# A streaming encoder layer on one core: output projection and second block finished tile by tile, projection weights loaded in quarters, and rope in four instructions

## The chip, the core and the metric

The kernel runs on one core of a Trainium2 chip. A core has a tensor engine (PE in the profile; PEld is its loading of weights), a vector engine (DVE), a scalar engine (ACT), a GpSimd engine (POOL), and queues for transfers, most of which here are issued by the sync engine (SP). The engines work each in their own order and wait for each other by semaphores. The metric is the device time of one execution in microseconds (us), as the median of several runs.

## What is computed

One step of a one-layer encoder for 1024 prompt rows and 64 sample rows, with 1024 columns, in float32:

```
def macaron_half(x, g, b, w_gate, w_up, w_down):
    return layer_norm(ALPHA * x + 0.5 * swiglu(x, w_gate, w_up, w_down), g, b)

hp = macaron_half(xp, ln1_g, ln1_b, ffn1_w_gate, ffn1_w_up, ffn1_w_down)
qa, ka, va, qi, ki, wi, qb, kb, vb, lfb = project(hp, pos_p, w_in, b_f)   # rope on qa, ka, qi, ki
mp = mixer_prompt(qa, ka, va, qi, ki, wi, qb, kb, vb, lfb)
hp = layer_norm(ALPHA * hp + mp @ w_out, ln2_g, ln2_b)
xp = macaron_half(hp, ln3_g, ln3_b, ffn2_w_gate, ffn2_w_up, ffn2_w_down)
```

The mixer has two groups of heads. Group A picks 256 keys per query by the scores of a small indexer (`relu(q_i . k_i)`, weighted) and attends to them; group B attends causally with a decay. The sample rows go the same way with a cache. The feed-forward blocks are 2816 wide. The outputs are the layer's rows and the new keys and values.

## The kernel before

The rows are held as nine tiles: t = 0 to 7 are 128 prompt rows each, t = 8 the 64 sample rows. To keep float32 precision, every operand of a product is split into a high part, a cast on ACT (L108), and a low part, a subtraction on DVE (L109). A product of two split operands takes three matmuls (high-high, high-low, low-high; `mm`, L113). A tile of rows is turned with PE transposes (`turned`, L124) before it is an operand.

The program runs through these stages: first block part a and part b (to about 741 us of the span), the input projections (to 1083), attention (to 1425), the output projection (to 1528), second block part a (to 2026), second block part b (to the end).

**Blocks.** Part a (`ffn_a`) computes gate and up, part b (`ffn_b`, L591) the down projection. Both use Strassen's scheme with seven half-size products; in part b they are P1 to P7, with P5, P7 and P4 last in that order. The inner dimension of each is cut into six PAIRS of up to 256, the last a half one. `load` (L628) fetches and splits a pair's two operands (`pair`, L621: `mh`, `ml` of the weight, `lh`, `ll` of the hidden rows), two pairs ahead, in rings of three. All tiles t = 0 to 3 use a pair before the next one, except for the last `late` pairs (three in P4, L710), which are done tile by tile, followed by the tile's `evict` (L674). In P4 with `last` (the second block) the eviction adds the product to the row (L662), runs the layer norm (`ln_tail`, L521 to L541) and writes the output.

**Strassen operands.** The second block's operands come from `Strassen.put` (L167): of tile t >= 4 and its partner t - 4 it forms differences (L175, L178, L179, L180 on GpSimd), turns them with PE into `xt` and splits them into T1 to T4 and B22. The partner's rows come back from DRAM into `zt` (`emit_s`, L1991), a 128x1024 buffer of the ring "wl" in the pool `wp`, which the weight splits use as well. The first product of the next stage, on the wide tile `fs`, needs them all.

**Output projection.** `gemm_b` (L432) takes the nine tiles in three groups of three. In a group all tiles go together through the inner dimension but for its tail; then each tile's tail is done in `order` (L435), followed by its first layer norm step. The remaining steps of the three (generators, of five turns each) are queued in `todo` in a fixed interleaving (L479) and are run as the next work is emitted (`pump`).

**Projections.** The 2888 columns of `w_in` are cut into eleven groups, stored as "w" (buffers `wh`, `wl` of the common rings) or as "p" (`iwh`, `iwl` of a pool of their own). `load_w` (L973) loads a group's weight in two parts ("w") or three ("p") into the ring "st" of three 128x1024 buffers and splits each at once (L975 cast on ACT, L976 subtraction). The ring "st" is also used by `rt`, the relu of the indexer scores (`idx_scores`, L1144, on ACT), which PE takes up again. `in_proj` (L1047) runs the tiles of a group and calls for the next group's weights at tile `ahead`. `proj_tile` copies the result to `ot` on ACT (L1040); its handler, run a little later, applies rope (`rope_apply`, L945, six instructions), turns the tile (`tsplit`, L1061, results `tsqb`, `tsqi`, with `hl` L1072 and `ft` L1078) and writes it out. The steps of the top-k search (`topk`, with `tk_bad`, L1327) run in between.

A scheduler orders the instructions of the engines from the order in which the code emits them; `tc.issue_after` pins a place. Queues work in their order: an instruction that waits holds those behind it on its engine.

## Time and profile before

| | us |
|---|---|
| median of 3 runs | 2279.86 (2279.32 to 2284.34) |
| the profiled execution | 2278.69 |
| its span, first to last instruction | 2276.9 |
| granted PE clock, mean | 0.982 of full speed |

The span is that of one execution, read by the hardware profiler. In the views, rows stand as start, duration, engine, line, operation and tiles; a bracket behind a row gives the idle time of the engine before it and what ended it. The table of waits gives the total, the number and the longest of each kind. The table of windows gives busy time by engine, then the granted PE clock, the share of the DMA engines and GB/s. Durations of rows overlap on pipelined engines, so that the step from one start to the next is what a row costs; the chain of waits lists these steps.

### The profile page before, as it was taken

How to read it: one execution, taken by the hardware profiler on the slowest of the kernel's cores; microseconds unless marked ns; L12 is line 12 of the kernel's file. 1: busy time of each engine (PE TensorE's matmuls, PEld its weight loads, DVE VectorE, ACT ScalarE, POOL GpSimd, SP SyncE). 2: the span in 40 equal slices, each digit the busy share in tenths (PEclk: the TensorE clock that was granted, in tenths of full speed). 3: DMA queues.
4: the chain of work that ended last, by engine and by line, in shares of the span. 5: the costliest groups of instructions: out<-in, count | busy, mean ns of one | idle time of the engine just before them, and what ended most of it. 6: DMA issues, size and time to landing. Idle time of an engine off the chain costs nothing.

```text
span 2276.9 us, 33875 instructions
## 1 busy us (share of the span) xinstructions
PE 2186.9 (96%) x11832; PEld 1878.7 (83%) x11832; DVE 1489.8 (65%) x2359; ACT 963.0 (42%) x1776; POOL 906.4 (40%) x1058
## 2 busy tenths in 40 slices
PE   8999999999999999999898999998999999999997
PEld 7888888887888989998897787886888888877886
DVE  4576675556569656686857887675555655654678
ACT  4333333334344356733666787333333333333332
POOL 4556556541011323352546655023564564530011
PEclk9999999999999999999999999998999999999999
DMA  6566544458556343554667533553443443477554
GB/s 200 180 210 217 186 153 148 140 178 304 166 196 208 108 121 118 161 151 133 171 172 202 146 93 113 166 183 113 149 160 117 158 156 117 159 258 237 179 182 152
DMA packets 330297, 379.31 MB, mean 167 GB/s; under 512 B 43440, under 2 KB 226160, under 8 KB 330124
## 3 DMA queue, kind: packets, MB, share of 16 engines
q1 hardware_dynamic: 330122, 377.13, 52.8%
q8 instruction: 94, 1.54, 0.3%
q14 instruction: 81, 0.65, 0.1%
HBM read 256.51 MB, written 120.53 MB: 166 GB/s over the span
## 4 chain that ended last, share of the span: by engine, by line
PE 45%; DVE 5%; issue 1%; ACT 1%; DMA 1%; POOL 1%; SPq 0%; DVEq 0%; ACTq 0%; POOLq 0%
PE fa L114 11%; PE fbP L114 8%; PE fz L114 5%; PE fy L114 3%; PE gb L114 3%; PE pq L114 2%; PE acc L114 2%; PE ip L114 2%; PE pt L1744 2%; PE fs L114 2%; DVE pp L109 1%; PE fbs L114 1%; PE gb_a L114 1%; PE gb_b L114 1%; PE sacc L114 1%
## 5 line engine op out<-in xcount | busy, mean ns | idle before, releaser
L114 PE MATMUL fbP<-ml,lh 128*128 128x512 f32 x616 | 238.6, 391 | 1.5 <-DVE ml L109 1.5
L114 PE MATMUL fbP<-mh,ll 128*128 128x512 f32 x616 | 237.9, 390 | 2.1 <-DVE ll L109 2.1
L108 ACT CAST wh<-wst 128x1024 fp32r<-128x1024 f32 x108 | 113.3, 1052 | 286.6 <-PE fs L114 108.6
L114 PE MATMUL fbP<-mh,lh 128*128 128x512 f32 x616 | 224.2, 392 | 2.6 <-ACT lh L108 1.7
L109 DVE TENSOR_TENSOR wl<-wst,wh 128x1024 fp32r<-128x1024 f32 x108 | 159.5, 1478 | 69.8 <-ACT wh L108 60.6
L331 DVE TENSOR_TENSOR Sl<-S,Sh 128x512 fp32r<-128x512 f32 x160 | 161.8, 1018 | 29.3 <-ACT Sh L330 27.7
L108 ACT CAST lh<-raw 128x1024 fp32r<-128x1024 f32 x84 | 82.4, 981 | 228.4 <-PE fbP L114 195.1
L662 POOL TENSOR_TENSOR zz<-u,zz 128x512 f32<-128x512 f32 x16 | 25.6, 1613 | 379.6 <-DVE u L684 268.8
L330 ACT CAST Sh<-S 128x512 fp32r<-128x512 f32 x160 | 97.4, 618 | 187.4 <-PE fa L114 113.9
L109 DVE TENSOR_TENSOR ll<-raw,lh 128x1024 fp32r<-128x1024 f32 x84 | 100.0, 1191 | 115.2 <-ACT lh L108 115.0
L327 POOL TENSOR_TENSOR S<-wst 128x512 f32<-128x512 f32 x80 | 125.1, 1564 | 113.5 <-DVE Sl L331 52.0
L327 POOL TENSOR_TENSOR S<-wst,S 128x512 f32<-128x512 f32 x40 | 61.6, 1539 | 239.0 <-issue 235.4
L114 PEld LDWEIGHTS fbP<-mh,lh 128*128 128x128 f32 x616 | 115.7, 189 | 27.7 <-ACT lh L108 2.0
L114 PEld LDWEIGHTS fbP<-ml,lh 128*128 128x128 f32 x616 | 115.5, 188 | 27.7 <-DVE ml L109 4.1
L114 PEld LDWEIGHTS fbP<-mh,ll 128*128 128x128 f32 x616 | 115.6, 188 | 26.8 <-DVE ll L109 2.9
L1681 POOL TENSOR_SCALAR e<-e,su 128x128 f32<-128x128 f32 (+7 forms) x128 | 99.4, 789 | 77.3 <-DVE su L1678 61.6
L114 PE MATMUL acc<-pp,vs 128*128 128x256 f32 (+1 forms) x640 | 114.8, 300 | 9.0 <-DVE pp L109 5.6
L109 DVE TENSOR_TENSOR pp<-pt,pp 128x512 fp32r<-128x512 f32 (+1 forms) x160 | 99.1, 631 | 29.4 <-ACT pp L108 28.0
L114 PE MATMUL ip<-iwh,xh 128*128 128x256 f32 (+3 forms) x384 | 114.7, 299 | 2.0 <-ACT o L1043 0.9
L114 PE MATMUL ip<-iwl,xh 128*128 128x256 f32 (+3 forms) x384 | 111.4, 290 | 0.0
L114 PE MATMUL ip<-iwh,xl 128*128 128x256 f32 (+3 forms) x384 | 111.3, 290 | 0.0
L114 PEld LDWEIGHTS acc<-pp,vs 128*128 128x128 f32 x640 | 91.1, 196 | 14.5 <-DVE pp L109 7.9
(507 smaller groups left out, 6746.9 us busy)
## 6 DMA issues: line engine op xcount, KB each, us to landing
wst<-ffn_w_gate SPq DMA_DIRECT2D x88, 256.0 KB
wst<-ffn_w_up SPq DMA_DIRECT2D x88, 256.0 KB
w<-ffn_w_down SPq DMA_DIRECT2D x44, 512.0 KB
raw<-ffn_w_down SPq DMA_DIRECT2D x40, 512.0 KB
wst<-w_out SPq DMA_DIRECT2D x24, 512.0 KB
hd0T<-w SPq DMA_DIRECT2D x44, 256.0 KB
hd0S<-ringz SPq DMA_DIRECT2D x44, 256.0 KB
hd1T<-w SPq DMA_DIRECT2D x44, 256.0 KB
```

The source lines that it names most:

```text
L108: S.copy(hi, src)
L109: V.tensor_tensor(lo, src, f(hi), ALU.subtract)
L114: last_mm[:] = [PE.matmul(out, lhsT, rhs, start=start, stop=stop, skip_group_check=more).ins]
L327: G.tensor_tensor(t, ss[0] if x is None else x, ss[1] if y is None else y, op)
L330: S.copy(hi, t)
L331: V.tensor_tensor(lo, t, f(hi), ALU.subtract)
L662: eng.tensor_tensor(z_of(t, d), acc, z_of(t, d), ALU.add)
L1681: G.tensor_scalar(es[q][:, :n], es[q][:, :n], su2[:, q:q + 1], 1.0, ALU.mult, ALU.mult)
L1744: PE.transpose(pt[:, m * P:(m + 1) * P], e[:, kt * P:(kt + 1) * P], ident)
```

## The change

It has these parts:

- `gemm_b` takes the last group's tiles in the order 0, 1, 2, and queues their layer norm steps tile by tile, five turns each.
- `put` works with `zt` as two halves of 128x512, and with a choice of engine. In `emit_s` the halves come from the ring "ssum" (four buffers of 128x512) by two transfers, and for tiles 6 and 7 the differences are formed on DVE.
- In `ffn_b` with `last`, the first four pairs of P4 are fetched and split into free slots of the large operand pool during P5 (pairs 0, 1) and P7 (pairs 2, 3). In P4 all six pairs are then done tile by tile.
- `rope_apply` multiplies all 16 rotated columns by cosine and by sine at once, and combines them with two instructions.
- `load_w` loads the weights of the nine 256- and 264-column groups in quarters of 128x2x256 (and one small remainder) into the ring "ssum". The loads are issued at once, the splits are kept in `wsp` and emitted one per tile from tile `ahead` + 2 on, the rest before the next group.
- `tsplit` alternates between the two kinds of PSUM tiles in the late groups, and one call of `in_proj` has `ahead` 5.

```diff
@@ -166,3 +166,3 @@
 
-        def put(self, t, z, hf, zt=None):
+        def put(self, t, z, hf, zt=None, E=G):
             if t == 8:
@@ -174,11 +174,11 @@
                 self.set("B22", t, turned(t, z, 1))
-                G.tensor_tensor(zt[:, 0:512], z[:, 0:512], zt[:, 0:512], ALU.subtract)
-                self.set("T1", t, turned(t, zt, 0))
+                E.tensor_tensor(zt[0], z[:, 0:512], zt[0], ALU.subtract)
+                self.set("T1", t, turned(t, zt[0], 0))
             else:
-                G.tensor_tensor(z[:, 0:512], z[:, 512:1024], z[:, 0:512], ALU.subtract)
-                G.tensor_tensor(z[:, 512:1024], z[:, 512:1024], zt[:, 0:512], ALU.subtract)
-                G.tensor_tensor(zt[:, 512:1024], zt[:, 512:1024], z[:, 512:1024], ALU.subtract)
+                E.tensor_tensor(z[:, 0:512], z[:, 512:1024], z[:, 0:512], ALU.subtract)
+                E.tensor_tensor(z[:, 512:1024], z[:, 512:1024], zt[0], ALU.subtract)
+                E.tensor_tensor(zt[1], zt[1], z[:, 512:1024], ALU.subtract)
                 self.set("T2", t, turned(t, z, 1))
                 self.set("T3", t, turned(t, z, 0))
-                self.set("T4", t, turned(t, zt, 1))
+                self.set("T4", t, turned(t, zt[1], 0))
 
@@ -434,3 +434,3 @@
             skew = tail if g == 2 else 2
-            order = (2, 0, 1) if g == 2 else (0, 1, 2)
+            order = (0, 1, 2)
             acc = []
@@ -478,3 +478,5 @@
                         pass
-            for j in (0, 0, 0, 1, 1, 1, 0, 0, 2, 2, 2, 1, 1, 2, 2):
+            turns = (0, 0, 0, 0, 0, 1, 1, 1, 1, 1, 2, 2, 2, 2, 2) if g == 2 else \
+                (0, 0, 0, 1, 1, 1, 0, 0, 2, 2, 2, 1, 1, 2, 2)
+            for j in turns:
                 if not last or g < 2:
@@ -623,3 +625,7 @@
                 st = fetch(src, n, tags[0])
-                hl = [pool.tile([P, 1024], F32R, tag=tg, name=tg, bufs=3) for tg in tags[1:]]
+                if pool is None:
+                    both = slot8("tl" + tags[1]).rearrange("p (s c) -> p s c", s=2)
+                    hl = [both[:, 0], both[:, 1]]
+                else:
+                    hl = [pool.tile([P, 1024], F32R, tag=tg, name=tg, bufs=3) for tg in tags[1:]]
                 split(hl[0][:, :n * 512], hl[1][:, :n * 512], st[:, :n * 512])
@@ -627,4 +633,8 @@
 
+            NP = len(PAIRS)
+            FAR = 4 if last else 0
+            far = [steps.index(("P4", q)) for q in range(FAR)]
+
             def load(i):
-                if i >= len(steps):
+                if i >= len(steps) or i in ops:
                     return
@@ -632,4 +642,5 @@
                 A, B = OPS[p]
-                ops[i] = pair(w_src(B, q), q, ("st", "mh", "ml"), hb_)
-                ops[i] += pair(hd[A][q][0:PAIRS[q][1]].rearrange("k p c -> p k c"), q, ("wl", "lh", "ll"), hb_)
+                pool = None if i in far else hb_
+                ops[i] = pair(w_src(B, q), q, ("st", "mh", "ml"), pool)
+                ops[i] += pair(hd[A][q][0:PAIRS[q][1]].rearrange("k p c -> p k c"), q, ("wl", "lh", "ll"), pool)
 
@@ -709,3 +720,3 @@
             for p in OPS:
-                late = 3 if p == "P4" else 2
+                late = (NP if last else 3) if p == "P4" else 2
                 acc = [sm(f"fb{p}_{t}") for t in range(4)]
@@ -715,2 +726,4 @@
                     load(i + q + 2)
+                    if last and p in ("P5", "P7") and q % 3 == 1:
+                        load(far[2 * (p == "P7") + q // 3])
                     if i + q == 2:
@@ -734,3 +747,6 @@
                     for q in range(len(PAIRS) - late, len(PAIRS)):
-                        product(acc[t], t, i + q, False, q == len(PAIRS) - 1)
+                        with ExitStack() as es:
+                            if last and p == "P4" and t and q == 0:
+                                es.enter_context(tc.issue_after(last_mm[0]))
+                            product(acc[t], t, i + q, q == 0, q == len(PAIRS) - 1)
                     evict(p, t, acc[t])
@@ -768,3 +784,3 @@
         def put(t, hf):
-            xo.put(t, at[t], hf, at.get(t - 4))
+            xo.put(t, at[t], hf, [at[t - 4][:, c * 512:(c + 1) * 512] for c in range(2)])
             yield
@@ -947,13 +963,11 @@
         v = ot[:r, c0:c0 + nh * HD].rearrange("p (h d) -> p h d", h=nh)
-        x1, x2 = v[:, :, 0:8], v[:, :, 8:16]
-        cosb = rope[:r, t, 0:1, :].to_broadcast([r, nh, 8])
-        sinb = rope[:r, t, 1:2, :].to_broadcast([r, nh, 8])
-        a, b = (att.tile([P, 4, 8], F32, tag=n, name=n, bufs=2) for n in ("ra", "rb"))
+        x12 = v[:, :, 0:16].rearrange("p h (s d) -> p h s d", s=2)
+        cosb, sinb = (rope[:r, t, q:q + 1, :].rearrange("p (a b) d -> p a b d", a=1).to_broadcast([r, nh, 2, 8])
+                      for q in range(2))
+        a, b = (att.tile([P, 4, 2, 8], F32, tag=n, name=n, bufs=2)[:r, :nh] for n in ("ra", "rb"))
         E = rp_[0]
-        E.tensor_tensor(a[:r, :nh], x1, sinb, ALU.mult)
-        E.tensor_tensor(b[:r, :nh], x2, sinb, ALU.mult)
-        E.tensor_tensor(x1, x1, cosb, ALU.mult)
-        E.tensor_tensor(x2, x2, cosb, ALU.mult)
-        E.tensor_tensor(x1, x1, b[:r, :nh], ALU.subtract)
-        E.tensor_tensor(x2, x2, a[:r, :nh], ALU.add)
+        E.tensor_tensor(a, x12, cosb, ALU.mult)
+        E.tensor_tensor(b, x12, sinb, ALU.mult)
+        E.tensor_tensor(x12[:, :, 0], a[:, :, 0], b[:, :, 1], ALU.subtract)
+        E.tensor_tensor(x12[:, :, 1], a[:, :, 1], b[:, :, 0], ALU.add)
 
@@ -972,2 +986,4 @@
 
+    wsp = []
+
     def load_w(c0, n, store, eng):
@@ -977,2 +993,20 @@
 
+        def later(dst):
+            rest = []
+            if n > 256:
+                ex = mp.tile([P, 512], F32, tag="hsh", name="wex")[:, 0:KD * (n - 256)].rearrange(
+                    "p (k c) -> p k c", k=KD)
+                DMA.dma_start(ex, w_in[:, c0 + 256:c0 + n].rearrange("(k p) c -> p k c", p=P))
+                rest.append((slice(0, KD), slice(256, n), ex))
+            for k in range(0, KD, 2):
+                st = mp.tile([P, 512], F32, tag="ssum", name="wst", bufs=4).rearrange("p (k c) -> p k c", k=2)
+                DMA.dma_start(st, w_in[k * P:(k + 2) * P, c0:c0 + 256].rearrange("(k p) c -> p k c", p=P))
+                rest.append((slice(k, k + 2), slice(0, 256), st))
+
+            def one(ks, cs, st):
+                hi, lo = dst(ks, cs)
+                sp2(hi, lo, st)
+
+            wsp.extend(lambda p=p: one(*p) for p in rest)
+
         if store == "w":
@@ -980,9 +1014,7 @@
             for u in range(2):
-                st = wp.tile([P, 1024], F32, tag="st", name="wst")
-                DMA.dma_start(st.rearrange("p (a b) -> p a b", a=4),
-                              w_in[u * 512:(u + 1) * 512, c0:c0 + n].rearrange("(k p) c -> p k c", p=P))
                 wh = wp.tile([P, 1024], F32R, tag="wh", name="wh")
                 wl = wp.tile([P, 1024], F32R, tag="wl", name="wl")
-                sp2(wh, wl, st)
                 us.append((wh, wl))
+            later(lambda ks, cs: [x.rearrange("p (k c) -> p k c", k=4)[:, ks.start % 4:ks.start % 4 + 2, cs]
+                                  for x in us[ks.start // 4]])
 
@@ -995,3 +1027,6 @@
             iwh = pw_[1].tile([P, KD, pw_[2]], F32R, tag="iwh", name="iwh")
-            for k0, kn in ((0, 2), (2, 2), (4, 2), (6, 2)) if hp_[0] is None else ((0, 3), (3, 3), (6, 2)):
+            if hp_[0] is not None and n < 328:
+                later(lambda ks, cs: (iwh[:, ks, cs], iwl[:, ks, cs]))
+            for k0, kn in ((0, 2), (2, 2), (4, 2), (6, 2)) if hp_[0] is None else \
+                    ((0, 3), (3, 3), (6, 2)) if n == 328 else ():
                 if hp_[0] is None:
@@ -1048,4 +1083,8 @@
         in_weights(gi)
+        while wsp:
+            wsp.pop(0)()
         for t in tiles:
             h = proj_tile(gi, t, mid)
+            if wsp and t > ahead + 1:
+                wsp.pop(0)()
             if t == ahead:
@@ -1060,4 +1099,7 @@
 
+    nts = [0]
+
     def tsplit(r, src, npair, scale, dst, c, cs, eng, name):
-        pt = (big if hp_[0] is pc else sm)("ts" + name)
+        nts[0] += 1
+        pt = (big if hp_[0] is pc and nts[0] % 2 else sm)("ts" + name)
         for q in range(npair):
@@ -1583,3 +1625,3 @@
     in_proj(0, (4, 5, 6, 7), -1)
-    in_proj(1, (4, 5, 6, 7), 6)
+    in_proj(1, (4, 5, 6, 7), 5)
     for gi in range(2, 4):
@@ -1613,2 +1655,4 @@
     hp_[0] = None
+    while wsp:
+        wsp.pop(0)()
     pend_9 = [proj_tile(9, t) for t in range(2)]
@@ -1995,7 +2039,9 @@
         if 4 <= t < 8:
-            zt = wp.tile([P, 1024], F32, tag="wl", name="zt")
-            DMA.dma_start(zt, h2d[t - 4])
-        xo2[0].put(t, z, 0, zt)
+            zt = [mp.tile([P, 512], F32, tag="ssum", name="zt", bufs=4) for _ in range(2)]
+            for c in range(2):
+                DMA.dma_start(zt[c], h2d[t - 4][:, c * 512:(c + 1) * 512])
+        E = V if t >= 6 else G
+        xo2[0].put(t, z, 0, zt, E)
         yield
-        xo2[0].put(t, z, 1, zt)
+        xo2[0].put(t, z, 1, zt, E)
```

What these do to the order of instructions is shown at three places. The first is ACT's order at the switch from the second to the third group of the projections. Before (`rt` is the relu of indexer scores, `iwh` the high part of a weight, `ist` its landing buffer):

```order
L1144 ACTIVATE rt<-iq_1_7380 128x640
L1040 COPY ot<-ip_2_7326 128x256
L1072 ACTIVATE hl<-tskb 128x2x128
L1078 ACTIVATE ft<-tskb 128x256
L975 CAST iwh<-ist 128x3x264 x2
L1144 ACTIVATE rt<-iq_2_7445 128x640
L975 CAST iwh<-ist 128x2x264
L1144 ACTIVATE rt<-iq_3_7462 128x640
```

Now:

```order
L991 CAST iwh<-wex 128x8x8
L991 CAST iwh<-wst 128x2x256 x2
L1114 ACTIVATE hl<-tsqi 128x2x128
L991 CAST iwh<-wst 128x2x256
L1152 CAST kid<-pk_7090 64x128
L991 CAST iwh<-wst 128x2x256
L1186 ACTIVATE rt<-iq_0_7115 128x384
```

The casts of the 264-column weight stood between the relus of 640 columns; now all of them stand ahead of the first relu.

The second place is the end of the operands of the second block, tile 7. Before, POOL formed its differences, with products of the first hidden columns (w) between:

```order
L180 TENSOR_TENSOR zt<-zt,zz 128x512
L245 TENSOR_TENSOR w_17420<-w_17420 128x512
L246 TENSOR_TENSOR w_17420<-w_17420 128x512
L247 TENSOR_TENSOR w_17420<-w_17420 128x512
L175 TENSOR_TENSOR zt<-zz,zt 128x512
L248 TENSOR_TENSOR w_17420<-w_17420 128x512
L178 TENSOR_TENSOR zz<-zz 128x512
L179 TENSOR_TENSOR zz<-zz,zt 128x512
L180 TENSOR_TENSOR zt<-zt,zz 128x512
```

Now they stand on DVE, between the splits (L109) of the turned parts:

```order
L175 TENSOR_TENSOR zt<-zz,zt 128x512
L109 TENSOR_TENSOR T4l<-xt_0_17045,T4h 128x4x128
L178 TENSOR_TENSOR zz<-zz 128x512
L109 TENSOR_TENSOR B22l<-xt_1_17091,B22h 128x4x128
L179 TENSOR_TENSOR zz<-zz,zt 128x512
L109 TENSOR_TENSOR T1l<-xt_0_17099,T1h 128x4x128
L180 TENSOR_TENSOR zt<-zt,zz 128x512
L109 TENSOR_TENSOR T2l<-xt_1_17121,T2h 128x4x128
L109 TENSOR_TENSOR T3l<-xt_0_17128,T3h 128x4x128
```

On SP's queue the copies of the partner's rows (h2d_91 for tile 6, h2d_92 for tile 7) now stand as halves between the writes of the tiles 6 (h2d_95), 7 (h2d_96) and the sample (h2d_97):

```order
L415 DMA wst<-ffn_w_up 128x4x128 x2
L2042 DMA zt<-h2d_91 128x512
L2037 DMA h2d_95<-zz 128x1024
L2042 DMA zt<-h2d_91 128x512
L2037 DMA h2d_96<-zz 128x1024
L2042 DMA zt<-h2d_92 128x512
L2037 DMA h2d_97<-zz 64x1024
L2042 DMA zt<-h2d_92 128x512
```

Before, the copy for tile 7 was one transfer behind all three writes and two loads of weights for the next product.

The third place is the end of the program on DVE. Before, the last steps of the tiles stood interleaved; these are its last rows but the closing branch:

```order
L539 SCALAR_TENSOR_TENSOR zz<-zz,bmv,gb 128x1024
L535 SCALAR_TENSOR_TENSOR bve<-brs,bve 128x1
L534 RECIPROCAL brs<-brs 128x1
L536 TENSOR_SCALAR bve<-bve 128x1
L535 SCALAR_TENSOR_TENSOR bve<-brs,bve 128x1
L537 TENSOR_TENSOR brs<-brs,bve 128x1
L536 TENSOR_SCALAR bve<-bve 128x1
L541 SCALAR_TENSOR_TENSOR zz<-zz,brs,gb 128x1024
L537 TENSOR_TENSOR brs<-brs,bve 128x1
L541 SCALAR_TENSOR_TENSOR zz<-zz,brs,gb 128x1024
```

Now the last rows are the chain of one tile (L673 was L662, L541 was L539, L543 was L541):

```order
L543 SCALAR_TENSOR_TENSOR zz<-zz,brs,gb 128x1024
L673 TENSOR_TENSOR zz<-fbP_3_22176,zz 128x512
L531 BN_STATS bst_22205<-zz 128x6
L532 BN_AGGR bmv<-bst_22205 128x2
L534 TENSOR_SCALAR bve<-bmv 128x1
L541 SCALAR_TENSOR_TENSOR zz<-zz,bmv,gb 128x1024
L536 RECIPROCAL brs<-brs 128x1
L537 SCALAR_TENSOR_TENSOR bve<-brs,bve 128x1
L538 TENSOR_SCALAR bve<-bve 128x1
L539 TENSOR_TENSOR brs<-brs,bve 128x1
L543 SCALAR_TENSOR_TENSOR zz<-zz,brs,gb 128x1024
```

The layer norm of each tile stands whole behind that tile's product, and the one before it is complete ahead of it.

## The prediction

> **What bounds the kernel now.** I read first the busy shares, then the table of what the tensor engine (PE) waited for, then windows around its longest waits, and last the rows inside those windows.
>
> ```profile
> PE 2186.9 (96%) x11832; PEld 1878.7 (83%) x11832; DVE 1489.8 (65%) x2359; ACT 963.0 (42%) x1776; POOL 906.4 (40%) x1058
> PE iq L114 <- ACT rt L1144: 4.7, 2, 4.5
> PE tsqb L1064 <- ACT ft L1078: 3.2, 2, 2.3
> PE xt L129 <- POOL zt L175: 5.6, 1, 5.6
> PE xt L129 <- POOL zz L179: 3.7, 2, 2.7
> PE tkf L114 <- DVE tk_bad L1327: 2.1, 1, 2.1
> ```
>
> PE is busy for 96% of the span: 90 us of 2276.9 are left, and no other engine is near its limit. The change takes no matmul away. It can gain only where PE stands still, or after PE's last matmul. The five waiting rows (total us, times, longest) are the single long stalls in the stretches that the change touches.
>
> ```profile
> core 0: us, PE busy (x) PEld busy (x) DVE busy (x) ACT busy (x) POOL busy (x), PEclk, DMA share, GB/s
> 741.00:1083.00 342.00, 328.14 (x2416) 315.19 (x2415) 230.72 (x517) 170.18 (x388) 127.91 (x315) 0.97 0.46 132
> 839.00:846.00 7.00, 6.17 (x27) 6.17 (x28) 4.96 (x6) 3.77 (x8) 0.00 (x0) 0.51 0.09 30
> 1023.40:1026.80 3.40, 3.40 (x16) 3.40 (x17) 3.40 (x6) 2.25 (x6) 3.39 (x1) 0.51 0.59 175
> 1037.00:1040.40 3.40, 3.16 (x15) 3.16 (x16) 0.54 (x4) 0.00 (x0) 0.00 (x0) 0.50 0.59 155
> 1562.70:1576.30 13.60, 7.15 (x32) 6.75 (x33) 4.71 (x7) 4.60 (x7) 7.21 (x6) 0.50 0.28 103
> 2171.00:2201.60 30.60, 30.60 (x136) 25.35 (x136) 18.95 (x21) 11.07 (x12) 3.46 (x2) 1.00 0.59 193
> 2201.60:2232.00 30.40, 30.03 (x133) 24.52 (x133) 29.93 (x54) 11.87 (x16) 1.92 (x2) 1.00 0.68 227
> 2232.00:2263.50 31.50, 31.31 (x137) 25.26 (x135) 24.19 (x36) 9.45 (x12) 4.07 (x3) 1.00 0.24 81
> 2263.50:2276.90 13.40, 0.00 (x0) 0.00 (x0) 9.82 (x25) 0.41 (x2) 0.00 (x0) 0.59 0.40 157
> ```
>
> The first row is the whole projection stage. Two things are to be seen below it. After each of the long stalls the granted clock is 0.5 for one window of 3.4 us or for several, so a stall costs itself and about half of PE's busy time in that window. And the last 13.4 us hold no matmul at all.
>
> The Trainium skill, "TensorE: Matmul & The Clock Gate", section "What's actually happening", says that the clock halves after a whole idle window of about 3.4 us. The windows here differ: the stalls of 2.3 and 2.1 us at 1023 and 1037 are followed by 0.51 and 0.50. By the page only the stalls of 4.5 and 5.6 us would carry a clock loss, which would make the sum below about 1 us smaller.
>
> **The change part by part.**
>
> *End of the second block (P4 tile by tile).* Rows of the chain of waits (start, us, engine), and two of the timeline:
>
> ```profile
> 2263.10 0.39 PE L114 MATMUL fbP<-mh,ll 128*128 128x512 f32 x1
> 2263.53 0.69 DVE L662 TENSOR_TENSOR zz<-fbP,zz 128x512 f32<-128x512 f32 x1
> 2208.05 1.10 DVE ml L109
> 2262.03 0.59 DVE zz L662
> 2262.81 0.60 DVE bst L529
> 2264.22 0.12 DVE bmv L530
> 2268.93 1.19 DVE zz L539
> 2272.07 1.28 DVE zz L541
> ```
>
> The last matmul ends at 2263.49. Before, the last three pairs of all four tiles run tile by tile, 15 matmuls each, so four layer norms pile up on DVE and its last step ends at 2273.35: a tail of 9.9 us after it. After, a tile's 33 matmuls stand together (33 x 0.227 = 7.5 us), and a tile's DVE chain is add 0.59, statistics 0.60, mean 0.12, four or five small steps of 0.06 to 0.12 (0.37), L539 1.19 and L541 1.28: with start gaps 4.3 us, shorter than a tile's 7.5. Three layer norms go beside matmuls, one stays: 9.9 - 4.3 = **5.6 us less**. The output DMA behind the last step (2273.35 to 2276.9) stays.
>
> Cover: each pair is two splits of 1.10 on DVE (row 2208). Pairs 0 and 1 of P4, split within P7 before, go into P5, which has room (18.95 of 30.6 busy, and 4.4 more). P7 takes pairs 2 and 3 in their place (4.4 for 4.4), and also pairs 4 and the half pair 5, which P4 split for itself before: 29.9 + 3.3 = 33.2 us of DVE work beside 30.4 of PE. P4, rid of 7.7 us of splits, can take the excess of 2.8; pair 5 is needed only at the end of a tile's 7.5 us. If the excess lands on PE all the same, it waits 2.8 us in P4 with a halved window after it, 1.7. So this part lies between 5.6 - 4.5 = 1 and 6 (small steps hidden too); I take 5.5, nearest to the chain's own rows.
>
> *Projections (quarters, deferred splits).* Rows of the timeline, with idle time and releaser in brackets:
>
> ```profile
> 836.11 0.85 ACT L975 CAST iwh<-ist 128x792 fp32r<-128x792 f32 x1 [2.40 <-DMA ist<-w_in]
> 838.32 0.85 ACT L975 CAST iwh<-ist 128x792 fp32r<-128x792 f32 x1 [1.35 <-DMA ist<-w_in]
> 839.08 0.70 ACT L1144 ACTIVATE rt<-iq 128x640 f32<-128x640 f32 x1
> 839.83 1.43 PE L114 MATMUL iq<-kid,qsi 128*128 128x384 f32 x4 [4.54 <-ACT rt L1144]
> 1023.22 1.06 ACT L975 CAST wh<-wst 128x1024 fp32r<-128x1024 f32 x1
> 1023.39 0.69 PE L1064 MATMUL tsqb<-ident,ot 128*128 128x128 f32 x2 [2.33 <-ACT ft L1078]
> 1031.28 0.83 ACT L975 CAST iwh<-ist 128x768 fp32r<-128x768 f32 x1 [2.89 <-DMA ist<-w_in]
> 1032.15 0.96 DVE L976 TENSOR_TENSOR iwl<-ist,iwh 128x768 fp32r<-128x768 f32 x1 [1.19 <-ACT iwh L975]
> 1037.24 0.37 PE L114 MATMUL tkf<-tk_bad,tk_ones 128*128 128x8 f32 x1 [2.06 <-DVE tk_bad L1327]
> ```
>
> At 836 ACT waits in order for a weight's DMA (2.40 + 1.35 us) while the relu of the indexer scores (rt), for which PE waits, stands behind it. The DMA is late because its buffer comes from the same three-buffer ring as rt. After, the weight's DMAs use four other buffers, and its casts stand some 35 ACT rows earlier, ahead of the first rt. The 4.54 us go, with half of the 6.17 busy us of the halved window: 7.6. Late next is rt itself, 0.70 per step.
>
> At 1031 ACT and DVE again wait for a weight part (2.89, 1.19), and the counting step tk_bad comes late behind them. With parts loaded long before, these waits go. 2.06 and 1.6 of clock are the whole stall; I take 2.5, since the count has its own DVE chain.
>
> At 1023 one cast of 1.06 stands ahead of the copy for which PE waits; after, four quarter casts do, half the size each, about 2.1 us in a row: 1 us worse. Bounds: from 1.7 better (its halved window no longer hit) to 2 worse; I take -1, nearest to the cast's row.
>
> Sum 7.6 + 2.5 - 1 = **9**, bounds 2 and 14, the upper with the 2.33 and its window gone. The 36 quarter loads take the place of two or three larger ones per group. They are issued at tile 2 and split from tile 4 on, one per tile; 342 us for ten groups of nine tiles is 3.8 us per tile, so 7.6 us lie between issue and the first split, 19 before the last. The Trainium skill, "DMA: Bandwidth & Descriptors", section "Rules for kernel authors", asks for 1 MiB or more per DMA, and its anatomy section fits 2.0 us fixed per transfer; by an estimate from that page four 256 KB loads in turn would take 10.4 us where two halves took 6.4. That speaks against quarters only if they do not overlap, which is the last rival below.
>
> *Rope with four instructions, alternating PSUM buffers, ahead 5 for 6.* They sit on DVE and POOL beside PE work. PE waits after rope are under 1 us each; I count 0, bounds -2 and +2.
>
> *Output projection end.*
>
> ```profile
> 1549.20 3.66 DVE L541 SCALAR_TENSOR_TENSOR zz<-zz,brs,gb 64x1024 f32<-64x1024 f32 x3
> 1534.78 5.51 PE fa L114 x24
> 1558.48 1.28 POOL zt L180
> 1560.53 4.50 DMA zt<-h2d
> 1566.48 1.13 PE xt L129 x4
> 1570.27 2.82 PE xt L129 x12
> 1573.09 5.30 PE fs L114 x32
> ```
>
> Three layer norms end together (x3, at 1552.86). Then POOL does four subtractions of 1.27 for tile 6, and only when tile 6's buffer is free (1560.53) does tile 7's copy start, 4.50 us of DMA, and four more POOL steps follow. PE idles 5.6 + 2.7 us there, and fs, the next work, starts at 1573.09, its first 3.2 us at half clock (to 1576.3), so 1.6 lost.
>
> After, tile 6 comes about 7 us earlier (its product is complete first and its turns are not interleaved), tile 7 at about 1551; the copies lie in a ring of four halves, so the 4.50 drops out; and the subtractions run on DVE at about 0.6 (the L662 pitch above) instead of 1.27. But DVE has also the splits of the transposed parts, one between every two subtractions (order rows in the section on the change), and the pair of late halves stands in SP's queue behind the sample's write. I put the last subtraction at about 1559.5, the last transposes at 1562. Then 24 fa matmuls, which PE had before to fill its waiting, follow (5.5), and fs starts at about 1569.5: 3.6 us earlier. A halved window is likely still there, since PE waits for DVE's steps in the meantime. **3.5 us less**; bounds -1 (late halves, clock) and 7 (clock whole, DVE quick).
>
> Sum: 5.5 + 9 + 0 + 3.5 = 18. The profiled execution took 2278.69 us (span 2276.9 and 1.8 around it); its place is 1.2 under the median of the runs shown, 2279.86. 2278.7 - 18 = 2260.7, by the median 2261.9. I say **2261**.
>
> **Rivals.**
>
> 1. *The projection's stall moves rather than goes* (the relu steps or the count are late by themselves): only 1.5 of the 9 come, 2278.7 - 5.5 - 3.5 - 1.5 = 2268. For it: rt's 0.70 steps run close to PE there. Against: ACT's bracket names the DMA.
> 2. *More at the output projection*: all idle and clock gone there, 7, and 12 in the projections: 2278.7 - 5.5 - 7 - 12 = 2254.
> 3. *DVE full in P7*, so that P4 waits: 5.5 becomes 1, 2278.7 - 1 - 9 - 3.5 = 2265. With rival 1 too, and no gain at the output projection: 2278.7 - 1 - 1.5 = 2276.
> 4. *Slower: quarter casts block ACT.* ACT works in order, and a quarter whose DMA has not landed holds the copies and relus behind it, as at 836. Each such group would cost a stall like that at 1023: 2.33 + 1.7 of clock = 4 us. Nine groups are deferred. The gains outside the projections are 9, so from three such groups on (12 against 9), with the old stalls not gone, it is slower; at six, 2278.7 - 9 + 24 = 2294. For it: four buffers only, transfers half as large. Against: 7.6 us and more between issue and use, and a DMA share of 0.46 in the stage's row.
>
> That the change does not do what it says is excluded for the order (the rows shown), not for its timing, which the rivals hold.
>
> **How the numbers follow.** Forecast 2261 (2255 to 2266): 0.58. Rival 1: 0.12. Rival 2: 0.12. Rival 3 alone: 0.06; with rival 1: 0.06, ending at no difference. Rival 4: 0.06. The range 2250 to 2273 holds the first four cases, with the bounds of the sum's terms, and leaves out the last two. 0.2% (4.6 us, about what a measurement of this kernel can tell from no change) puts the border at 2275.3: faster 0.88, same 0.06, slower 0.06.
>
> **What would show it.** Right: no PE wait over 1 us for rt near 836; the last L543 within 5 us of the last matmul; no DMA wait on zt near 1560, fs started by 1570. Wrong: brackets with DMA on the deferred casts (L991); PE waiting for ll or ml inside P4; a DVE row without gaps from P7 on; a halved window where none was.

## The result and the profile after

| | before, us | after, us |
|---|---|---|
| median | 2280.62 (4 runs, 2279.32 to 2284.34) | 2263.74 (4 runs, 2262.34 to 2267.00) |
| span of the profiled execution | 2276.9 | 2260.5 |

The ratio after to before is 0.9932, with a 95% interval from 0.9913 to 0.9951: 15.5 us faster by the ratio, 16.9 by the medians, 16.4 by the spans. A second set of five runs gave 0.9936 (0.9919 to 0.9953), 13.7 us by the medians.

The same table of PE's waits as before, now of the changed kernel (total us, times, longest), with its busy shares:

```profile
PE 2185.0 (97%) x11832; PEld 1875.8 (83%) x11832; DVE 1495.5 (66%) x2361; ACT 964.4 (43%) x1791; POOL 890.7 (39%) x971
PE xt L129 <- DVE bve L538: 3.4, 1, 3.4
PE ip L114 <- DVE hl L1116: 3.3, 2, 1.9
PE xt L129 <- DVE zt L175: 2.8, 2, 2.4
PE iq L114 <- ACT rt L1186: 2.2, 3, 1.7
```

The single waits of 4.5 us for `rt` and of 5.6 us for `zt` are gone, the longest that are left in these stretches are 3.4 and 2.4, and those at the operands of the second block now name DVE instead of POOL. Windows over whole stages give what each is worth. Columns: stretch, length, busy time of PE, PEld, DVE, ACT and POOL, then the granted clock, DMA share and GB/s. The borders are PE's first matmul of the projections (`ip`), of the attention (`pq`) and of the output projection (`gb`), the last one of the latter, and the first of part b (`fbP`). Before (projections, attention, second block part a with the operands ahead of it):

```profile
750.39:1070.48 320.09, 306.88 (x2285) 296.16 (x2283) 216.41 (x486) 160.87 (x364) 120.82 (x272) 0.96 0.45 130
1070.48:1424.85 354.37, 325.23 (x2276) 292.03 (x2274) 268.79 (x607) 246.44 (x606) 201.09 (x368) 0.97 0.56 153
1528.00:2026.14 498.14, 485.68 (x2319) 405.86 (x2316) 289.23 (x349) 156.48 (x247) 253.36 (x174) 0.99 0.44 143
```

After (the same three, then P7 and P4 of the second block):

```profile
749.87:1060.02 310.15, 301.38 (x2284) 291.07 (x2283) 218.36 (x475) 160.94 (x375) 118.00 (x225) 0.98 0.44 129
1060.02:1415.15 355.13, 327.52 (x2273) 293.35 (x2271) 265.84 (x605) 245.64 (x604) 196.88 (x336) 0.96 0.56 153
1519.09:2014.78 495.69, 486.87 (x2320) 407.44 (x2318) 287.73 (x350) 156.35 (x246) 245.29 (x166) 0.98 0.43 143
2190.40:2220.80 30.40, 30.04 (x133) 24.54 (x132) 30.40 (x53) 15.77 (x21) 1.27 (x2) 1.00 0.62 208
2220.80:2251.60 30.80, 30.57 (x134) 24.67 (x132) 26.62 (x46) 1.28 (x5) 5.70 (x4) 1.00 0.22 86
```

From these and the stage borders the 16.4 us of the span are: ahead of the projections 0.5, projections 9.9, attention 0.8 lost, output projection 0.8 lost, operands and part a 2.5, part b to the last matmul 0.6, the tail behind it 4.7, and the last write 0.3 lost. So the second block (5.3 for a term of 5.5) and the projections (9.9 for 9) came close to their terms, and the operands brought 2.5 for 3.5. The 0.5 is no gain: over the fourteen profiled executions of this study, the stretch ahead of the projections took 748.1 to 753.8 us.

Rows of the timeline of the changed kernel, at the third group of the projections and (the last two) near its end:

```profile
813.33 1.14 ACT L991 CAST iwh<-wst 128x512 fp32r<-128x512 f32 x2
815.31 0.62 ACT L991 CAST iwh<-wst 128x512 fp32r<-128x512 f32 x1
815.83 0.86 ACT L1186 ACTIVATE rt<-iq 128x384 f32<-128x384 f32 x2
818.96 0.62 ACT L991 CAST wh<-wst 128x512 fp32r<-128x512 f32 x1 [1.06 <-DMA wst<-w_in]
819.80 0.62 ACT L991 CAST wh<-wst 128x512 fp32r<-128x512 f32 x1 [0.22 <-DMA wst<-w_in]
821.27 0.99 PE L114 MATMUL iq<-kid,qsi 128*128 128x384 f32 x4 [1.75 <-ACT rt L1186]
1019.18 0.62 ACT L991 CAST iwh<-wst 128x512 fp32r<-128x512 f32 x1 [2.00 <-DMA wst<-w_in]
1022.78 0.62 ACT L991 CAST iwh<-wst 128x512 fp32r<-128x512 f32 x1 [2.33 <-DMA wst<-w_in]
```

The casts that had held `rt` back are done before the first `rt`. The two casts at 819 belong to the next group: they wait for their transfers (1.06 + 0.22) in front of relus, and PE waits 1.75 us. It is the same kind of stall as the 4.54 before, only short, and no halved window follows it. At 1019 and 1022 deferred casts wait for their transfers again, 2.00 and 2.33 us, but PE then has other work: between 822 and 1043 it has no wait over 0.7 us.

The end of the operands and of the program, same view, and then the chain of waits at the operands:

```profile
1540.77 1.27 DVE L543 SCALAR_TENSOR_TENSOR zz<-zz,brs,gb 128x1024 f32<-128x1024 f32 x1
1542.79 1.94 PE L129 MATMUL xt<-ident,zz 128*128 128x128 f32 x8 [3.37 <-DVE bve L538]
1549.22 1.09 PE L129 MATMUL xt<-ident,zz 128*128 128x128 f32 x4 [1.31 <-DVE zz L179]
1549.59 0.68 DVE L180 TENSOR_TENSOR zt<-zt,zz 128x512 f32<-128x512 f32 x1
2251.55 0.69 DVE L673 TENSOR_TENSOR zz<-fbP,zz 128x512 f32<-128x512 f32 x1 [2.40 <-PE fbP L114]
2255.35 1.28 DVE L543 SCALAR_TENSOR_TENSOR zz<-zz,brs,gb 128x1024 f32<-128x1024 f32 x1
```

```profile
1551.16 4.70 PE fa L114 x12
1555.86 0.45 PE xt L129 x4
1557.46 5.76 PE fa L114 x24
1563.22 2.87 PE fs L114 x24
```

Neither DVE nor PE waits for a copy of the partner's rows (`zt`) any more; DVE's last difference (1549.59) lies 30.5 us behind the end of the output projection (1519.09), where POOL's lay 42.3 behind it before (1570.29 - 1528.0). At the end DVE waits for PE (2.40) ahead of the last tile: its norm is the only one behind the last matmul, 2251.55 to 2256.63, 5.1 us where there were 9.9.

### The profile page after: what moved, and what is told of

It reads as the page before. It is cut to its first block, busy times and chain, and to the rows that moved or that the text cites. A ratio compares the mean times of both kernels' runs of the same rounds, so it can differ in the third digit from the quotient of the medians.

```text
span 2260.5 us, 33816 instructions
## 1 busy us (share of the span) xinstructions
PE 2185.0 (97%) x11832; PEld 1875.8 (83%) x11832; DVE 1495.5 (66%) x2361; ACT 964.4 (43%) x1791; POOL 890.7 (39%) x971
## 5 line engine op out<-in xcount | busy, mean ns | idle before, releaser
L114 PE MATMUL fbP<-ml,lh 128*128 128x512 f32 x584 | 226.4, 391 | 1.9 <-DVE ml L109 1.7
L114 PE MATMUL fbP<-mh,ll 128*128 128x512 f32 x584 | 225.7, 390 | 2.1 <-DVE ll L109 2.1
L114 PE MATMUL fbP<-mh,lh 128*128 128x512 f32 x584 | 212.3, 391 | 3.3 <-ACT lh L108 1.7
L109 DVE TENSOR_TENSOR wl<-wst,wh 128x1024 fp32r<-128x1024 f32 x108 | 159.4, 1477 | 64.9 <-ACT wh L108 61.4
L673 POOL TENSOR_TENSOR zz<-u,zz 128x512 f32<-128x512 f32 x16 | 26.6, 1674 | 380.3 <-DVE u L695 268.1
L109 DVE TENSOR_TENSOR ll<-raw,lh 128x1024 fp32r<-128x1024 f32 x80 | 95.5, 1194 | 107.7 <-ACT lh L108 107.6
L114 PEld LDWEIGHTS fbP<-ml,lh 128*128 128x128 f32 x584 | 109.5, 188 | 27.1 <-DVE ml L109 4.8
L114 PEld LDWEIGHTS fbP<-mh,lh 128*128 128x128 f32 x584 | 109.2, 188 | 27.3 <-ACT mh L108 3.0
L114 PEld LDWEIGHTS fbP<-mh,ll 128*128 128x128 f32 x584 | 109.7, 188 | 25.5 <-DVE ll L109 2.9
L109 DVE TENSOR_TENSOR pp<-pt,pp 128x512 fp32r<-128x512 f32 (+1 forms) x160 | 99.3, 632 | 31.7 <-ACT pp L108 30.9
L1788 PE MATMUL pt<-ident,e 128*128 128x128 f32 x576 | 93.6, 283 | 8.2 <-DVE pp L109 4.3
```

The source lines that it names most:

```text
L109: V.tensor_tensor(lo, src, f(hi), ALU.subtract)
L114: last_mm[:] = [PE.matmul(out, lhsT, rhs, start=start, stop=stop, skip_group_check=more).ins]
L673: eng.tensor_tensor(z_of(t, d), acc, z_of(t, d), ALU.add)
L1788: PE.transpose(pt[:, m * P:(m + 1) * P], e[:, kt * P:(kt + 1) * P], ident)
```

## Experiments

**1. Each part alone on the kernel before.** Four kernels take over one part each; the diffs are the pieces of the change shown above.

The output-projection part (`gemm_b`, `put`, `emit_s`):

```diff
-            order = (2, 0, 1) if g == 2 else (0, 1, 2)
+            order = (0, 1, 2)
...
+        E = V if t >= 6 else G
+        xo2[0].put(t, z, 0, zt, E)
```

> The kernel before with the output-projection part alone (tile order and turns, copies in halves from the four-buffer ring, differences of tiles 6 and 7 on DVE). Theory, parts add: from the end of the output projection's matmuls to the first matmul of the second block's part b the trace of the changed kernel is 2.4 us shorter than before (1519.1 to 2014.8 against 1528.0 to 2026.1); the same is expected here, time 2280.6 - 2.4 = 2278, and PE still waits over 2 us for DVE steps at the last operands. Rival, the gain at this place came from other parts (earlier weights, the free ring): no gain, 2280 to 2281.

Measured: ratio 1.0001 (0.9990 to 1.0011). In its profile the stretch from the output projection's last matmul to part b took 495.0 us against 498.1, so the 2.4 us are there and more, and PE still waits 2.37 and 3.83 us for DVE, as expected. The timed runs do not settle it: the ratio's interval ends at 2.3 us of gain, and the medians differ by 2.0 (2277.44 against 2279.46).

P4 tile by tile (`ffn_b`):

```diff
+            FAR = 4 if last else 0
...
+                late = (NP if last else 3) if p == "P4" else 2
```

> The kernel before with P4 of the second block done tile by tile alone, first four pairs ahead. Theory, parts add: the DVE tail after the last matmul falls from 9.9 to 5.1 us as in the changed kernel, and PE inside P5, P7 and P4 loses nothing: 2280.6 - 5 = 2275.5. Rival, part of it needs the other parts (an earlier or fuller clock): tail the same but PE waits in P4, 2277 to 2280.

Measured: ratio 0.9981 (0.9968 to 0.9994), 4.3 us. The tail is 5.11 us as in the changed kernel, and PE waits no more than 0.15 us in P4, so that the rival did not come. The span of its profiled execution, though, was 1.1 us longer than before, since the projections took 323.0 us instead of 320.1 and the attention 357.5 instead of 354.4 (row of the windows):

```profile
1073.46:1430.96 357.50, 331.58 (x2276) 298.31 (x2275) 269.04 (x607) 246.78 (x606) 201.05 (x368) 0.94 0.56 152
```

Up to P5 of the second block the instructions of this kernel and of the one before stand in the same order on PE, DVE, ACT and POOL. The same 2276 matmuls of the attention took 331.6 busy us at a clock of 0.94 here and 325.2 at 0.97 there. So the difference does not come from the order of the instructions. It goes with how many windows of 3.4 us were granted at half clock, 41 us in all here and 24 there; why they differ is open.

The deferred quarters (`load_w` with `later`, `in_proj`):

```diff
+            wsp.extend(lambda p=p: one(*p) for p in rest)
...
+            if wsp and t > ahead + 1:
+                wsp.pop(0)()
```

> The kernel before with the deferred quarter loads of the projection weights alone (rope and PSUM alternation as before). Theory: the waits of 4.5 us for rt and of 2.1 us for tk_bad go with their half-clock windows, the projections are 8 to 10 us shorter, 2280.6 - 9 = 2271.5. Rival, rope and the alternating PSUM tiles carry a share of it: 4 to 6 us shorter, 2275 to 2277.

Measured: ratio 0.9978 (0.9964 to 0.9992), 5.0 us; projections 314.1 us, 6.0 shorter, which is the rival's 4 to 6. The median, 2272.44, is 7.0 us lower, between the two. The wait for `rt` came out 2.26 us long (1.75 in the changed kernel), and this time a halved window followed. So it is not settled whether rope and PSUM carry the rest: experiment 2 finds projections of 309.5 and 311.0 us with either of them undone. PE's row in the timeline:

```profile
823.60 1.33 PE L114 MATMUL iq<-kid,qsi 128*128 128x384 f32 x3 [2.26 <-ACT rt L1169]
```

The window behind it, with its clock of 0.59:

```profile
823.00:826.50 3.50, 2.90 (x11) 2.90 (x12) 2.60 (x4) 2.29 (x6) 1.28 (x1) 0.59 0.89 273
```

Rope and the alternating PSUM tiles:

```diff
+        E.tensor_tensor(a, x12, cosb, ALU.mult)
+        E.tensor_tensor(b, x12, sinb, ALU.mult)
...
+        pt = (big if hp_[0] is pc and nts[0] % 2 else sm)("ts" + name)
```

> The kernel before with rope in four instructions and alternating PSUM tiles alone. Theory: beside other work, within 1 us of before, 2280.6; the wait of 4.5 us for rt at the third group stays. Rival, they carry a share of the projections' gain: 2275 to 2277.

Measured: ratio 0.9994 (0.9982 to 1.0007), nothing that can be told. The wait for `rt` stays at 4.07 us. The waits of 2.3 and 2.1 us near 1023 and 1037 shrank, and a new one took their place, behind a weight's cast that waits 2.13 us for its transfer and the subtraction that follows it on DVE:

```profile
836.43 0.85 PE L114 MATMUL iq<-kid,qsi 128*128 128x384 f32 x4 [4.07 <-ACT rt L1145]
1031.71 0.43 PE L1065 MATMUL tsqa<-ident,ot 128*128 128x128 f32 x2 [4.75 <-DVE ot L956]
```

By the centres of the four ratios the parts give 0.46% together, the whole change 0.68%; the intervals (about 0.13% each, 0.19% for the whole) let these be the same. By the medians (2279.46 before; 2277.44, 2274.80, 2272.44 and 2276.81 with one part each) the parts give 16.4 us together, the whole 16.9. Whether the parts add up exactly cannot be told.

**2. One thing undone in the changed kernel.** First the six instructions of rope back:

```diff
-        E.tensor_tensor(a, x12, cosb, ALU.mult)
-        E.tensor_tensor(b, x12, sinb, ALU.mult)
...
+        E.tensor_tensor(a[:r, :nh], x1, sinb, ALU.mult)
+        E.tensor_tensor(b[:r, :nh], x2, sinb, ALU.mult)
```

> The changed kernel with rope in six instructions again. Theory: rope is hidden beside other work; projections as long as in the changed kernel (310.2 us in its profile) to within a half-clock window or two (1.7 us each), time 2264 to 2266. Rival, rope itself carries 2 us or more: projections 312 us or more with new waits of PE for rope's rows, 2266 to 2268.

Measured: ratio 0.9923 (0.9902 to 0.9944), not different from the changed kernel. Projections 311.0 us against 310.2. The wait for `rt` was 2.71 us here, with a halved window behind it. The shorter rope carries nothing that these runs can see.

Then the turned tiles without alternation:

```diff
-        pt = (big if hp_[0] is pc and nts[0] % 2 else sm)("ts" + name)
+        pt = (big if hp_[0] is pc else sm)("ts" + name)
```

> The changed kernel with the turned tiles of the late groups all in the large PSUM tiles again. Theory: the alternation took away the waits of 2.3 and 0.9 us for ft and hl near 1023 to 1035, for which I had expected a loss; without it PE waits there again for hl or ft, 1.5 to 3 us in all and a halved window, projections 312 to 314, time 2266 to 2268. Rival: no difference, those waits went with the casts, 2264.

Measured: ratio 0.9953 (0.9939 to 0.9968), 2.1 thousandths over the changed kernel's with overlapping intervals; the median, 2267.94, lies in the theory's range. The trace speaks for the rival: its projections took 309.5 us, no longer than the changed kernel's, the wait near 1023 did not come back, and no halved window stood there. So those waits went with the casts. Its attention took 358.7 us. Whether the alternation is worth something elsewhere stays open.

Then the quarters without deferral:

```diff
-            wsp.extend(lambda p=p: one(*p) for p in rest)
+            for p in rest:
+                one(*p)
```

> The changed kernel with the quarters split as soon as they are called for, not one per tile. Theory A, the gain comes from the other ring, which the relu tiles do not use: the wait of 4.5 us for rt stays away, time within 2 us of the changed kernel, 2264 to 2266. Theory B, deferral is needed: casts that wait for their transfer hold rt and the copies back, waits of 2 to 4 us with halved windows return, 2270 or more.

Measured: ratio 0.9947 (0.9928 to 0.9966); median 2267.47, between the two theories; projections 314.1 us, 4.0 longer. Both theories hold in part. The wait for `rt` stays short (1.87 us), so that one was cured without the deferral, by the quarters in a ring of their own (no run separates their size from their ring). But the splits again wait for their transfers, and with them the steps behind them on DVE, those of rope and of the top-k search's count. In this kernel's timeline, ACT, DVE and PE:

```profile
1029.06 1.35 ACT L991 CAST iwh<-wst 128x512 fp32r<-128x512 f32 x2 [1.75 <-DMA wst<-w_in]
1030.96 0.62 ACT L991 CAST iwh<-wst 128x512 fp32r<-128x512 f32 x1 [0.55 <-DMA wst<-w_in]
1031.61 0.69 DVE L992 TENSOR_TENSOR iwl<-wst,iwh 128x512 fp32r<-128x512 f32 x1 [0.40 <-ACT iwh L991]
1033.54 0.41 PE L1107 MATMUL tsqa<-ident,ot 128*128 128x128 f32 x2 [3.04 <-DVE tk_nw L1369]
```

And the window behind the 3.04 us, at a clock of 0.62:

```profile
1034.00:1038.50 4.50, 4.36 (x24) 4.36 (x25) 0.51 (x4) 0.00 (x0) 0.06 (x1) 0.62 0.41 118
```

So the part has two effects: the quarters in their ring shorten the stall for `rt`, and the deferral takes away the one behind the late splits near 1031. In the kernel before, the count (`tkf`) met that one with 2.06 us; here it is the transposes of a rotated tile, as in the kernel with rope and PSUM alone (4.75 us). Each is read from one profiled execution.

**3. The operands taken apart.** The order and turns alone on the kernel before:

```diff
-            order = (2, 0, 1) if g == 2 else (0, 1, 2)
+            order = (0, 1, 2)
...
+            turns = (0, 0, 0, 0, 0, 1, 1, 1, 1, 1, 2, 2, 2, 2, 2) if g == 2 else \
```

> The kernel before with the order 0, 1, 2 and the turns by tile alone at the output projection (differences on GpSimd, whole copies). Theory: the differences of tile 6 start earlier, but tile 7's copy of 4.5 us still waits for tile 6's buffer and ends last: from the last matmul of the output projection to part b 497 us, as before to within 1. Rival, the order is the gain: 495.

Measured in one execution: from the last matmul of the output projection to part b 502.6 us, 4.5 more than before. Neither theory. The chain of waits of this kernel shows why:

```profile
1553.42 1.29 DVE zz L543
1555.24 4.82 DMA w<-ffn_w_down
1560.19 1.29 POOL w L245
1563.27 3.90 DMA zt<-h2d
1567.31 1.26 POOL zt L175
1571.31 3.88 PE xt L129 x20
1578.04 4.94 PE fa L114 x12
```

POOL's products for the hidden columns (`w`) stand here ahead of tile 7's differences, and their own transfer of 4.82 us ends the chain's way to them; the copy of 3.90 us follows on that. PE waited 6.54 us at 1568.62, and 20 us ran at half clock.

The copies in halves and the differences on DVE alone (order 2, 0, 1 and interleaved turns as before):

```diff
+            zt = [mp.tile([P, 512], F32, tag="ssum", name="zt", bufs=4) for _ in range(2)]
...
+        E = V if t >= 6 else G
```

> The kernel before with the copies in halves and the differences of tiles 6 and 7 on DVE alone (order 2, 0, 1 and interleaved turns as before). Theory: the 4.5 us copy goes from the chain, but both tiles still end their layer norms together, so eight steps of 0.6 us and as many splits follow them on DVE: 496. Rival, the order matters nothing: 495.

Measured in one execution: 499.2 us, 1.1 more than before, and again neither theory. Tile 7's halves still land too late:

```profile
1562.58 0.69 DVE L175 TENSOR_TENSOR zt<-zz,zt 128x512 f32<-128x512 f32 x1 [1.13 <-DMA zt<-h2d]
1563.42 0.63 PE L129 MATMUL xt<-ident,zt 128*128 128x128 f32 x4 [3.48 <-DVE zt L175]
```

Either half of the part alone was no gain in its one execution; together they took 495.0 (on the kernel before) and 495.7 (in the changed kernel). Four profiled executions without the part took 496.1, 497.0, 497.1 and 498.1; six with it took 492.9 to 495.7. By the means the part is worth 2.5 us in the traces (497.1 - 494.6).

**4. A version that goes further.** DVE has hardly a gap from 1528 to 1550 in the changed kernel. First only tile 6's differences back on POOL:

```diff
-        E = V if t >= 6 else G
+        E = V if t >= 7 else G
```

> The changed kernel with the differences of tile 6 on GpSimd again, tile 7 on DVE. Theory: DVE, which has no gap from 1528 to 1550, is the bound at the last operands, and the four differences of tile 6 taken from it (2.4 us) let tile 7 come 1.5 to 2.4 us earlier: 2261.5 to 2262.5. Rival: the chain of 1.27 us steps on GpSimd is late itself and PE waits for it, 2264 to 2266.

Measured: ratio 0.9932 (0.9909 to 0.9954), as the changed kernel; the median, 2264.88, is in the rival's range. The stretch took 493.7 us, 2.0 less than in the changed kernel's profile, inside the spread of kernels with the part. PE now waits for POOL, as the rival had it:

```profile
1546.04 1.26 POOL L179 TENSOR_TENSOR zz<-zz,zt 128x512 f32<-128x512 f32 x1
1547.38 2.26 POOL L180 TENSOR_TENSOR zt<-zt,zz 128x512 f32<-128x512 f32 x1
1547.36 1.59 PE L129 MATMUL xt<-ident,zz 128*128 128x128 f32 x8 [3.53 <-POOL zz L179]
```

Then also the last normalisation step and its write in two halves:

```diff
+            for hf in range(2):
+                cs = slice(hf * 512, (hf + 1) * 512)
+                V.scalar_tensor_tensor(z[:r, cs], z[:r, cs], rs[:r], bt[:r, cs], ALU.mult, ALU.add)
+                cut(cs)
```

> The changed kernel with tile 6's differences on GpSimd, and the very last normalisation step in two halves, each followed by its own write of the output. Theory: 1.3 us less up to part b of the second block (493.7 against 495 us, seen already for tile 6), and 0.6 to 1 us less behind the last matmul, since the first half's write starts 0.6 us earlier and the second one moves half as much: 1.5 to 2 us under the changed kernel. Rival, a write's time does not hang on its size and the second write starts when the one write did: only 1 us, not to be told from nothing.

The changed kernel, unedited, ran beside it:

> The changed kernel itself once more, beside the next run on the same chip. Both theories: ratio to before 0.993 (0.991 to 0.995), the gain of 15.5 to 17 us is not one of the first chip alone; its projections about 310 us, the attention 353 to 359 by the number of halved windows in it.

Measured for the halved end: median 2261.45 (5 runs), ratio 0.9918 (0.9902 to 0.9935), and for the changed kernel 2265.56 and 0.9936 (0.9919 to 0.9953), as in its first runs; its projections took 307.7 us and its attention 358.9. The halved end is the fastest of the study by its median, 4.1 us under the changed kernel where 1.5 to 2 were expected, but the intervals overlap. From the last matmul to the end it took 8.41 us where the changed kernel took 8.98 (5.12 + 3.86): 0.6 us, the low end of what was expected. Its attention was the slowest of the fourteen:

```profile
1062.16:1421.65 359.49, 333.23 (x2272) 299.21 (x2270) 267.55 (x605) 245.94 (x604) 197.49 (x336) 0.94 0.56 151
```

## Why the prediction came out

The forecast was 2261, the measurement 2263.7. The mechanisms held where most of the gain lies; that the sum came so near is in part luck, since the attention, which the sum leaves out, took 355.1 to 359.5 us in the seven profiled executions with the whole change or nearly so, and the first of them, at 355.1, lost least. Step by step:

- **Second block, 5.5:** the tail lost 4.7 us and part b 0.6 (with this part alone, part b came out 1.0 longer, so the 0.6 may be chance). The term was right in sum, its size wrong inside: I had 4.3 us for the one remaining norm, it takes 5.1. In a chain of one tile every step waits for the one before it, so that even the smallest steps start 0.19 to 0.26 us apart: the four from L536 (2254.51) to L543 (2255.35) take 0.84 us, where I had 0.37 for all of them, and the add, the statistics and the mean take 1.70 where I had 1.31. The interleaved chains of before hid that. The cover held: DVE was full in P7 (30.40 of 30.40), the excess went into P4 (26.62 of 30.8), and PE waited 0.2 us there. DVE without gaps in P7 was one of my signs of being wrong; it came and cost nothing. The rival, that P4 would wait for it, did not come.
- **Projections, 9:** 9.9 in the first execution, 12.4 in the second. The mechanism was right and the place of one step wrong. The wait for `rt` went from 4.54 to 1.75, and its two halved windows went; the count's wait went too (in experiment 2, without the deferral, a wait of 3.04 us comes back near that place). I had expected the wait at 1023 to stay and to grow by 1 us; it went too. In its place come waits for `hl` (3.3 us, two) behind steps of the top-k search on DVE, which I had not foreseen. My sign "no PE wait over 1 us for rt" failed by those 1.75 us, for the reason that the last rival gives: a cast that waits for its transfer ahead of a relu. A DMA bracket on L991, one of my signs of being wrong, came at 1019 and 1022 too. The rival itself did not come, since PE has other work there. The fixed 2.0 us that I took from the Trainium skill ("DMA: Bandwidth & Descriptors", the section on the anatomy of one DMA) is a fit for transfers that GpSimd issues. The loads here are issued by SP, so that my estimate of 10.4 against 6.4 us did not fit them; no run shows what a quarter's transfer costs by itself.
- **Rope and PSUM, 0:** nothing that the runs can tell, by experiments 1 and 2; for the alternation this is open by 2.1 thousandths.
- **Output projection, 3.5:** 2.5. Tile 7's layer norm and its last difference came where I had put them: 1540.77 and 1549.59 are 1549.7 and 1558.5 on the clock of before (plus 8.9), for an expected 1551 and 1559.5. The step that failed lies between that difference and the last transposes. They came at 1555.86 in the chain, which is 1564.8 on that clock, not 1562, since 12 more matmuls of the first hidden columns stand ahead of them, at half clock (4.70 us). The 24 that I counted follow as forecast (5.76 us), so `fs` came at 1563.22, 1572.1 on that clock, not 1569.5, and my sign "fs started by 1570" failed. But these 12 are work that PE need not do later, so `fs` is no measure of the gain. The stretch itself tells it: PE's idle time went from 12.5 to 8.8 us, halved windows took 2.3 us more (they start at 1538.17 now, where there were none), and the rest came out 1.1 less, 2.4 in all.
- **Not in the sum:** 0.8 us lost in the output projection itself, whose 103.2 became 104.0, in every profiled execution with the quarters and in both of experiment 3. In the changed kernel four more of the attention's last matmuls fall behind the border (14 `acc` for 10), which is part of it; the rest of the cause was not sought.

## What to carry to other kernels

A stage's length is worth splitting into PE's idle time, its busy time lost to the halved clock, and a rest. In the projections that rest was 295.8 to 296.9 us in all fourteen profiled executions, while the stage went from 308 to 323. When an engine that works in order stands behind a transfer, a ring of its own for the transfer and a later place for its consumer are two means, and here they cured different waits. The later place need not end the consumer's wait; it is enough that nothing PE needs stands behind it. When two halves of a change are each no gain, they may still be one together, if either alone only leaves the other's transfer as the last to come.

## What was not expected of the hardware

The halved clock varies between executions by more than most parts of this change gain. The attention held 20 to 44 us at half clock in the fourteen profiled executions (in windows that are all multiples of about 3.4), at idle times between 26 and 30 us, and its length ran from 353.3 to 359.5, mostly with it; two kernels with the same order of instructions there took 354.4 and 357.5. In the projections, 24 us at half clock before became 10 in both executions of the changed kernel. In the first of them a loss of 11.0 us became 4.9; this makes 6 of its 10 us, and PE's idle time, 13.2 to 8.8, the other 4.

Whether a halved window follows a wait is not fixed by the wait's length. In the eight profiled executions with quarters, the waits for `rt` of 1.57, 1.87, 1.92, 2.26 and 2.71 us were followed by one, those of 1.73, 1.75 and 1.85 were not.

The seven profiled executions with the whole change or nearly so had the longer attention, 357.7 us on the mean against 354.7 in the seven others. Whether the change does that, or chance, stays open; if it does, it costs about 3 us that the prediction did not count.
